# Loads of q and gates moved from ScalarE's to SyncE's queue, and the reload of the activation blocks spread over 24 projection steps, in a hybrid attention and retention layer

## The chip, the cores and the metric

The kernel runs on one core of a Trainium2 chip. The metric is device time in microseconds (us) of one execution; a time is the median of several. PE is TensorE, PEld its weight loads, DVE VectorE, ACT ScalarE, POOL GpSimd, SP SyncE. SPq and ACTq are the queues from which SyncE and ScalarE issue transfers.

## What is computed

One layer on 2048 latent tokens (a 32 x 64 grid) with 256 context tokens, width 1024. After an RMSNorm and a modulation, one input projection gives eight groups of columns: q, k, v and gate of a neighbourhood attention (8 heads of 64), and q, k, v and gate of a bidirectional retention (4 heads of 128). Both results are multiplied by their gates, joined, projected once more and added to the input.

```python
na_q, na_k, na_v, na_g, r_q, r_k, r_v, r_g = _split_proj(h_lat @ w_in)
o_na = _neighbourhood_attention(_heads(na_q, NA_HEADS), _heads(na_k, NA_HEADS),
                                _heads(na_v, NA_HEADS), k_na_ctx, v_na_ctx, na_rpb)
y_na = _merge(o_na) * jax.nn.silu(na_g)
o_ret = o_f + jnp.flip(o_b, 2)
y_ret = _head_rmsnorm(o_ret, ret_norm_g).astype(dt) * jax.nn.silu(r_g)
y_lat = jnp.concatenate([y_na, y_ret], axis=-1) @ w_out
x = x + gate * y_lat
```

In the attention each latent query reads, in one softmax, a clamped window of 8 rows and 16 columns of the grid with a learned bias, and all context keys.

## The kernel before

Products are made in float32r from two parts, a rounded value ("hi") and its remainder ("lo"), in three matmuls. The normalised activations h lie in five blocks: four of 512 latent tokens, and one of 256 context tokens. Each block has a tile `hhi` and a tile `hlo`.

The program has four stages. First the projections of the attention and part of the retention run block by block (`tform`, line 351, and `tokform`, line 361); their results go to DRAM (qS, kS, vS, vB, gS, and rkS, rvS, rqS for the retention). Blocks 2 and 3 of h are written to DRAM as well (hS), because their space is needed. Then comes the attention, tile by tile, with the remaining retention projections woven in. After it come the backward states of the retention, and last the forward retention with the output projection.

The attention loop (line 964) has 128 tiles, t = 16h + 4i + j: head h, block of eight grid rows i, block of sixteen columns j, and three more rounds at its end. One round makes the scores of tile t (`s_mm`, PE, line 755), their minimum with the bias (`s_min`, DVE, line 764), the exponential (`s_exp`, ACT, line 769), the normalisation of tile t−1 (`s_norm`, POOL, line 775), the transposes of tile t−2 into `tr` (`p_tr`, PE, lines 782 and 784), the copy of `tr` into `pt` (ACT, line 786) and its remainder (DVE, line 792), and the product of tile t−3 with v (`pv`, PE, lines 803 and 805). Every second tile is put together by `combine` (lines 826 to 834). On every fourth tile it multiplies by the gate `gt` on POOL and stores the result y in yS.

Between these steps stands `fill` (line 703). It advances a stream of projection steps, of which a unit (u_rk, u_rv, u_rq) has eight and ends with a store. Over the whole loop 384 − 66 = 318 such steps are shared out evenly among the 131 rounds; the 66 are held back for the stage behind. Each call of a step first takes one entry off the list `dmas` and issues it on SyncE; an entry may be `None`. `reload(b)` (line 622) fills this list with the loads of a block from hS: it is called for block 2 when the last step of the u_rq units of block 0 is done, and for block 3 after block 1, in the third pair of weight groups (line 691). From there 32 steps (two u_rk units and two u_rq units) pass before block b+2 is read.

At the end of each round loads for later tiles are issued: the q of the next row block (`load_q`, line 723, two buffers, two transfers each) at j = 0; the gate (`load_gate`, line 813, two buffers) at j = 1; groups of v (`load_v`, line 730, six buffers); the bias (`bias`, line 737, into `nb`); k and the context's v of the next head (`load_head`, line 715). The q of the next head is loaded at i = 3, j = 0. All of them go out on SyncE, but for q and the gate, which ACT issues. Stores go out on ACT too (line 149, put off by one or two rounds). The weights of the stream come into `st` (line 175), the rotary tables into `rot` (lines 402 and 405), both on SyncE.

The order of the instructions on an engine is that of the code. An engine that issues a transfer waits in its place until the transfer may go; what stands behind on that engine waits with it. The builder gives the transfers of both queues eight completion semaphores in turn, DMAHW0 to DMAHW7.

Of the kernel before, what the change touches and what calls it, by code (L numbers as in the profile page):

```python
# [81 lines left out]
def hybrid_kernel(ctx: ExitStack, tc: tile.TileContext, a: dict, out: bass.AP):  # L82
    nc = tc.nc
    f = lambda ap: ap[:].bitcast(F32)
# [6 lines left out]
    gS = [dram.tile([P, L], F32, name=f"gS{t}") for t in range(4)]  # L91
# [6 lines left out]
    hS = [[dram.tile([P, KC * 512], F32, name=f"hS{b}_{hl}") for hl in range(2)] for b in range(2)]  # L98
# [40 lines left out]
    def tick():  # L139
        for e in later:  # L140
            e[0] -= 1
        due = [e for e in later if e[0] <= 0]
        later[:] = [e for e in later if e[0] > 0]
        for e in due:
            e[1]()
# [10 lines left out]
    blk = [(hx.tile([P, KC, 512], F32R, name="hhi"), hx.tile([P, KC, 512], F32R, name="hlo"))] + [None] * 4  # L156
# [463 lines left out]
    dmas, chop = [], []  # L620

    def reload(b):
        blk[b] = (hx.tile([P, KC, 512], F32R, name="hhi"), hx.tile([P, KC, 512], F32R, name="hlo"))
        dmas.extend([None] * 3)
        for k in range(0, KC, 2):
            for hl in range(2):
                dmas.append((f(blk[b][hl])[:, k:k + 2, :].rearrange("p k t -> p (k t)"), hS[b - 2][hl][:, k * 512:(k + 2) * 512]))

    def fill_stream(w):
        def units(kind, b):  # L630
# [51 lines left out]
        for b in range(4):  # L682
            for n, args in enumerate(units(rk, b)):
                yield from steps(rk(w, ck, *args))
                late_load(n + 2 * b)
            if b == 3:
                w = next_c()
            for args in units(rq, b):
                yield from steps(rq(wn, cq, *args))
            if b < 2:  # L690
                reload(b + 2)
# [11 lines left out]
    def fill(n):  # L703
        for _ in range(n):
            if dmas:
                d = dmas.pop(0)
                if d:
                    nc.sync.dma_start(*d)
            if next(env["fill"], 0) == 0:
                return  # L710
# [12 lines left out]
    def load_q(hd, h, i):  # L723
        q = kp.tile([P, 2, 512], F32R, name="q", bufs=2)
        src = qS[h // 2][i, 64 * (h % 2):64 * (h % 2) + 64]
        for e in range(2):
            nc.scalar.dma_start(f(q)[64 * e:64 * e + 64], src)
        hd["q"][i] = q

    def load_v(hd, gs):  # L730
        for g in gs:
            vt, h = kp.tile([P, 4, P], F32R, name="vt", bufs=6), hd["h"]
            for e, n in ((0, P), (2, 96)):
                nc.sync.dma_start(f(vt)[:n, e:e + 2, :], vB[h // 4][:n, g, e:e + 2, (h % 4) * P:(h % 4 + 1) * P])
            hd["vt"][g] = vt

    def bias(h, rt, ct):
        n, o = BT[rt][ct]
        nc.sync.dma_start(nbz[int(rt == 1)][:, nbt[int(rt == 1), ct]:][:, :n], a["rpb_t"][h, :, o:o + n])
# [3 lines left out]
    def dims(t):  # L743
        h, i, j = t // 16, t // 4 % 4, t % 4
        return h, i, j, KWIN[i][0], KWIN[i][1], CWIN[j][0], CWIN[j][1]

    def s_mm(t):
        h, i, j, kr0, kr, kc0, cw = dims(t)
        hd, nk, odd = heads[h], kr * cw, t % 2
        pl = sS[:, 1024:1024 + nk] if odd else sS[:, 512 - nk:512]  # L750
        pc = sS[:, 768:1024] if odd else sS[:, 512:768]
        kg = hd["k2"][:, :L].rearrange("p (r c) -> p r c", c=GW)
        for o, k in ((pl, kg[:, kr0:kr0 + kr, kc0:kc0 + cw]), (pc, hd["k2"][:, L:])):
            for hl in range(2):
                nc.tensor.matmul(o, hd["q"][i][:, hl, j * P:(j + 1) * P], k, start=(hl == 0), stop=(hl == 1))  # L755
        tl_st[t] = dict(s=sS[:, 768:1024 + nk] if odd else sS[:, 512 - nk:768], nk=nk, lo=LC * odd, co=nk * (1 - odd),
                        sp=ap_.tile([P, 768], F32, name="sp", bufs=3), st=ap_.tile([P, 4], F32, name="stt", bufs=4))

    def s_min(t):
        h, i, j = dims(t)[:3]  # L760
        T = tl_st[t]
        n, big = T["nk"] + LC, int(RTYPE[i] == 1)
        o = nbt[big, CTYPE[j]] - T["lo"]
        nc.vector.tensor_tensor_reduce(T["sp"][:, :n], T["s"], nbz[big][:, o:o + n], -1.0, 3e38, ALU.add, ALU.min, T["st"][:, 0:1])  # L764

    def s_exp(t):
        T = tl_st[t]
        sp, st, n = T["sp"], T["st"], T["nk"] + LC
        nc.scalar.activation(sp[:, :n], sp[:, :n], AF.Exp, bias=st[:, 0:1], scale=-1.0, accum_out=st[:, 1:2])  # L769

    def s_norm(t):
        T = tl_st[t]
        sp, st, n = T["sp"], T["st"], T["nk"] + LC
        nc.vector.reciprocal(st[:, 2:3], st[:, 1:2])  # L774
        nc.gpsimd.tensor_scalar(sp[:, :n], sp[:, :n], st[:, 2:3], 0.0, ALU.mult, ALU.add)  # L775

    def p_tr(t):
        h, i, j, kr0, kr, kc0, cw = dims(t)
        T = tl_st[t]
        sp, nk, ng_, cn = T["sp"], T["nk"], kr // 4, 4 * cw  # L780
        for g in range(ng_):
            nc.tensor.transpose(tr[:cn, g, :], sp[:, T["lo"] + g * cn:T["lo"] + (g + 1) * cn], ident)  # L782
        for g in range(2):
            nc.tensor.transpose(tr[:, ng_ + g, :], sp[:, T["co"] + g * P:T["co"] + (g + 1) * P], ident)  # L784
        pt = ap_.tile([P, 6, 2, P], F32R, name="pt")
        nc.scalar.copy(pt[:, :ng_ + 2, 0, :], tr[:, :ng_ + 2, :])  # L786
        T.update(pt=pt, ng=ng_)

    def p_lo(t):
        T = tl_st[t]  # L790
        pt, n = T["pt"], T["ng"] + 2
        nc.vector.tensor_tensor(pt[:, :n, 1, :], tr[:, :n, :], f(pt)[:, :n, 0, :], ALU.subtract)  # L792
# [15 lines left out]
    gts = {}  # L808

    def fin_(h):  # L810
        return slice(0, 64) if h % 2 == 0 else slice(64, 128)

    def load_gate(t):
        h, i = dims(t)[:2]
        gts[t // 4] = ap_.tile([P, 512], F32, name="gt", bufs=2)
        nc.scalar.dma_start(gts[t // 4][fin_(h)], gS[h // 2][fin_(h), i * 512:(i + 1) * 512])

    def combine(t):
        h, i, j = dims(t)[:3]
# [47 lines left out]
    def decay_exp(dcol, c128):  # L867
        lg = rt["lg"]
        nc.scalar.activation(lg, lg, AF.Exp)
        nc.vector.tensor_scalar(lg, lg, -1.0, None, ALU.mult)  # L870
        for H in HS:
            for d in range(2):
                sc = lg[:, d * RH + H["r"]:d * RH + H["r"] + 1]
                nc.scalar.activation(H["w"][:, d:d + 1], dcol[:, d:d + 1], AF.Exp, scale=sc)
                nc.scalar.activation(H["w"][:, 2 + d:3 + d], c128, AF.Exp, scale=sc)
# [88 lines left out]
    for t in range(NT + 3):  # L964
        if t == 6:
            decay_exp(*dec)
        quota = (NF - held) * (t + 1) // (NT + 3) - done
        done += quota
        part = [quota // 3 + (quota % 3 > n) for n in range(3)]
        tick()  # L970
        if t < NT:
            s_mm(t)
        if 0 <= t - 1 < NT:
            s_norm(t - 1)
        fill(part[0])
        if t < NT:
            s_min(t)
        if 0 <= t - 2 < NT:
            p_tr(t - 2)
        if t < NT:  # L980
            s_exp(t)
        if 0 <= t - 2 < NT:
            p_lo(t - 2)
        fill(part[1])
        if 0 <= t - 3 < NT:
            pv(t - 3)
            if (t - 3) % 2 == 1:
                combine(t - 3)
        fill(part[2])
        if t >= NT:  # L990
            continue
        h, i, j = dims(t)[:3]
        hd = heads[h]
        if i == 0 and j < 3:
            bias(h, 1, j)
        if i == 2 and j < 3:
            bias(h, 2, j)
        if j == 1:
            load_gate(t)
        if i < 3 and j == 0:  # L1000
            load_q(hd, h, i + 1)
        for g in {(0, 2): (3,), (0, 3): (4,), (1, 1): (5,), (1, 3): (6,), (2, 3): (7,)}.get((i, j), ()):
            load_v(hd, (g,))
        if h + 1 < NH:
            if i == 1 and j == 2:
                heads[h + 1] = load_head(h + 1)
            if i == 3:
                nh = heads[h + 1]
                if j == 0:
                    load_q(nh, h + 1, 0)  # L1010
                if j == 1:
                    bias(h + 1, 0, 0)
                    load_v(nh, (0,))
                if j == 3:
                    bias(h + 1, 0, 1)
                    load_v(nh, (1, 2))
        if h > 0 and (i, j) == (0, 0):
            bias(h, 0, 2)
# [211 lines left out]
    q, r = divmod(48 - used, 7)  # L1230
    plan = [q + (n < r) for n in range(7)] + [15] * 8 + [10] * 4
    for s in range(NJ + 3):
        q = plan[s]
# [121 lines left out]
```

## Time and profile before

| | us |
|---|---|
| median of 3 runs (lowest, highest) | 1401.06 (1400.52, 1403.14) |
| the profiled execution | 1401.82 |
| its span, first to last instruction | 1400.0 |
| PE busy | 1346.2 |
| DVE busy | 641.3 |
| ACT busy | 530.9 |
| POOL busy | 493.3 |

The profile is that of one execution. A line of the timeline has start and length in us, engine, source line, operation, tile written and tiles read, partitions x elements, and count; the bracket at its end is the time that the engine stood idle before it, with what ended that. SPq and ACTq rows are transfers issued; their length is that of the issue, not of the transfer. In the chain of waits each row has start and length of one step of the chain that ended last; a DMA row there lasts from issue to landing. The granted clock of TensorE is a share of full speed, and the DMA share is the mean busy share of the core's 16 DMA engines.

### The profile page before, as it was taken

Reading aid. Unit: us, or ns where it says so; the run is one execution under the profiler, and the core shown is the slowest. Engines: PE = TensorE matmul, PEld = TensorE weight load, DVE = VectorE, ACT = ScalarE, POOL = GpSimd, SP = SyncE. Lnnn points to the kernel's source line nnn. Section 1 sums busy time; section 2 is a strip of 40 time slices with the busy share of each in tenths; the row PEclk is TensorE's granted clock in tenths of the full one; section 3 lists DMA queues with packets and bytes.
Section 4 is the critical chain, followed back from the end, with each engine's and each line's share of the span. In section 5 each row is a group of like instructions: output and inputs, shape, how many; then the busy total and the mean of one; then the engine's idle time right before and its main releaser. Section 6 shows DMA issues by size and latency. Waiting matters only on the chain.

```text
span 1400.0 us, 22749 instructions
## 1 busy us (share of the span) xinstructions
PE 1346.2 (96%) x8380; PEld 1176.6 (84%) x8380; DVE 641.3 (46%) x1244; ACT 530.9 (38%) x1155; POOL 493.3 (35%) x499
## 2 busy tenths in 40 slices
PE   6999999999999999999999998899999999999997
PEld 2477899988887888899899898798999779888886
DVE  5787211100021131467776766676663643344445
ACT  4454312122112121555556544346552234333332
POOL 4352402022110221344554433346343155454342
PEclk9999999999999999999999999999999999999999
DMA  9543578743154678758768696966636898555533
GB/s 312 171 151 121 191 251 276 223 136 105 48 170 132 217 259 265 201 151 209 207 166 213 190 276 183 257 182 172 185 110 224 269 312 269 183 167 172 158 114 128
DMA packets 218705, 270.45 MB, mean 193 GB/s; under 512 B 16865, under 2 KB 163425, under 8 KB 217570
## 3 DMA queue, kind: packets, MB, share of 16 engines
q1 hardware_dynamic: 175106, 184.30, 44.3%
q10 hardware_dynamic: 43488, 84.69, 18.8%
q8 instruction: 67, 1.10, 0.3%
q14 instruction: 44, 0.36, 0.1%
HBM read 179.80 MB, written 89.13 MB: 192 GB/s over the span
## 4 chain that ended last, share of the span: by engine, by line
PE 77%; DMA 8%; DVE 6%; issue 3%; ACT 2%; POOL 2%; SPq 1%; ACTq 0%; POOLq 0%; DVEq 0%
PE mm L357 25%; PE mm L368 19%; PE mm L1199 12%; PE sS L755 4%; PE tr L782 3%; PE po L803 3%; PE mm L922 2%; PE mm L301 2%; PE tr L784 2%; PE po L805 1%; DMA q<-qS 1%; DMA hlo<-hS 1%; DMA vt<-vB 1%; DMA v<-rvS 1%; PE mm L1111 1%
## 5 line engine op out<-in xcount | busy, mean ns | idle before, releaser
L357 PE MATMUL mm<-hhi,whi 128*128 128x512 f32 x640 | 260.3, 407 | 0.0
L357 PE MATMUL mm<-hlo,whi 128*128 128x512 f32 x640 | 254.0, 397 | 5.4 <-DVE hlo L254 2.1
L357 PE MATMUL mm<-hhi,wlo 128*128 128x512 f32 x640 | 254.0, 397 | 0.2 <-DVE wlo L338 0.2
L368 PE MATMUL mm<-whi,hhi 128*128 128x256 f32 x768 | 224.2, 292 | 0.0
L368 PE MATMUL mm<-wlo,hhi 128*128 128x256 f32 x768 | 216.7, 282 | 2.7 <-POOL wlo L338 2.7
L368 PE MATMUL mm<-whi,hlo 128*128 128x256 f32 x768 | 215.5, 281 | 0.0
L338 POOL TENSOR_TENSOR wlo<-st,whi 128x256 fp32r<-128x256 f32 (+1 forms) x97 | 112.1, 1171 | 243.2 <-ACT whi L336 240.2
L786 ACT CAST pt<-tr 128x640 fp32r<-128x640 f32 (+1 forms) x128 | 95.6, 747 | 201.8 <-PE tr L784 167.6
L792 DVE TENSOR_TENSOR pt<-tr,pt 128x640 fp32r<-128x640 f32 (+1 forms) x128 | 113.9, 890 | 104.9 <-ACT pt L786 104.1
L368 PEld LDWEIGHTS mm<-wlo,hhi 128*128 128x128 f32 x768 | 144.6, 188 | 3.4 <-POOL wlo L338 3.3
L357 PEld LDWEIGHTS mm<-hlo,whi 128*128 128x128 f32 x640 | 121.2, 189 | 30.8 <-issue 2.5
L357 PEld LDWEIGHTS mm<-hhi,whi 128*128 128x128 f32 x640 | 121.1, 189 | 29.5 <-issue 5.4
L357 PEld LDWEIGHTS mm<-hhi,wlo 128*128 128x128 f32 x640 | 120.8, 189 | 29.5 <-DVE wlo L338 0.6
L368 PEld LDWEIGHTS mm<-whi,hlo 128*128 128x128 f32 x768 | 144.9, 189 | 0.0
L368 PEld LDWEIGHTS mm<-whi,hhi 128*128 128x128 f32 x768 | 144.8, 189 | 0.0
L775 POOL TENSOR_SCALAR sp<-sp,stt 128x640 f32<-128x640 f32 (+2 forms) x128 | 103.2, 808 | 113.2 <-DVE stt L774 76.8
L764 DVE CUSTOM_DVE_ANT_0 sp<-sS,nb 128x640 f32<-128x640 f32 (+2 forms) x128 | 105.6, 825 | 21.8 <-PE sS L755 14.0
L769 ACT ACTIVATE sp<-sp,stt 128x640 f32<-128x640 f32 (+2 forms) x128 | 107.5, 839 | 15.4 <-DVE stt L764 15.0
L755 PE MATMUL sS<-k,q 128*128 128x256 f32 (+3 forms) x512 | 99.0, 315 | 4.6 <-DVE stt L764 4.2
L1199 PE MATMUL mm<-wor,y 128*128 128x512 f32 x384 | 95.9, 398 | 0.9 <-DVE xt L1208 0.7
L755 PEld LDWEIGHTS sS<-k,q 128*128 128x128 f32 x512 | 83.8, 189 | 11.4 <-DVE stt L764 6.6
L1199 PE MATMUL mm<-won,y 128*128 128x512 f32 x336 | 89.9, 406 | 0.0
(214 smaller groups left out, 2238.5 us busy)
## 6 DMA issues: line engine op xcount, KB each, us to landing
st<-in_w_in_dram SPq DMA_DIRECT2D x48, 512.0 KB
q<-qS ACTq DMA_DIRECT2D x64, 256.0 KB
k<-kS SPq DMA_DIRECT2D x16, 576.0 KB
kS<-o SPq DMA_DIRECT2D x16, 512.0 KB
woS<-g ACTq DMA_DIRECT2D x32, 256.0 KB
qS<-o ACTq DMA_DIRECT2D x16, 512.0 KB
vt<-vB SPq DMA_DIRECT2D x64, 128.0 KB
k<-rkS SPq DMA_DIRECT2D x32, 256.0 KB
```

The source lines that it names most:

```text
L338: eng.tensor_tensor(l, r, f(h), ALU.subtract)
L357: nc.tensor.matmul(pm[:, :n], ww[:, k, cs], h[:, k, :], start=(k == 0 and i == 0), stop=(k == KC - 1 and i == 2))
L368: nc.tensor.matmul(pm[:, t * WG:(t + 1) * WG], h[:, k, o:o + P], ww[:, k, :], start=(k == 0 and i == 0), stop=(k == KC - 1 and i == 2))
L755: nc.tensor.matmul(o, hd["q"][i][:, hl, j * P:(j + 1) * P], k, start=(hl == 0), stop=(hl == 1))
L764: nc.vector.tensor_tensor_reduce(T["sp"][:, :n], T["s"], nbz[big][:, o:o + n], -1.0, 3e38, ALU.add, ALU.min, T["st"][:, 0:1])
L769: nc.scalar.activation(sp[:, :n], sp[:, :n], AF.Exp, bias=st[:, 0:1], scale=-1.0, accum_out=st[:, 1:2])
L775: nc.gpsimd.tensor_scalar(sp[:, :n], sp[:, :n], st[:, 2:3], 0.0, ALU.mult, ALU.add)
L782: nc.tensor.transpose(tr[:cn, g, :], sp[:, T["lo"] + g * cn:T["lo"] + (g + 1) * cn], ident)
L786: nc.scalar.copy(pt[:, :ng_ + 2, 0, :], tr[:, :ng_ + 2, :])
L792: nc.vector.tensor_tensor(pt[:, :n, 1, :], tr[:, :n, :], f(pt)[:, :n, 0, :], ALU.subtract)
L803: nc.tensor.matmul(po[:, t % 2, :, :], hd["vt"][kr0 // 4 + g][:cn, VORD.index(j), :], pt[:cn, g, :, :], start=(g == 0), stop=False)
L1199: nc.tensor.matmul(pm, yy[:, k, :], ww[:, k, sl], start=(k == 0 and i == 0), stop=(k == 3 and i == 2))
```

## The change

Three things change. The two transfers of `load_q` and that of `load_gate` are issued by SyncE. `reload` puts two empty entries ahead of each of its eight pieces, in place of three ahead of the first: the pieces go out at steps 3, 6, ... 24 after the call, where they went out at steps 4 to 11. And at the end of a round the q load stands first, ahead of the bias, while the gate's load stands behind the v groups and is issued one tile later, at j = 2.

```diff
     def reload(b):
         blk[b] = (hx.tile([P, KC, 512], F32R, name="hhi"), hx.tile([P, KC, 512], F32R, name="hlo"))
-        dmas.extend([None] * 3)
         for k in range(0, KC, 2):
             for hl in range(2):
-                dmas.append((f(blk[b][hl])[:, k:k + 2, :].rearrange("p k t -> p (k t)"), hS[b - 2][hl][:, k * 512:(k + 2) * 512]))
+                dmas.extend([None, None, (f(blk[b][hl])[:, k:k + 2, :].rearrange("p k t -> p (k t)"), hS[b - 2][hl][:, k * 512:(k + 2) * 512])])
...
         for e in range(2):
-            nc.scalar.dma_start(f(q)[64 * e:64 * e + 64], src)
+            nc.sync.dma_start(f(q)[64 * e:64 * e + 64], src)
...
-        nc.scalar.dma_start(gts[t // 4][fin_(h)], gS[h // 2][fin_(h), i * 512:(i + 1) * 512])
+        nc.sync.dma_start(gts[t // 4][fin_(h)], gS[h // 2][fin_(h), i * 512:(i + 1) * 512])
...
+        if i < 3 and j == 0:
+            load_q(hd, h, i + 1)
         if i == 0 and j < 3:
             bias(h, 1, j)
         if i == 2 and j < 3:
             bias(h, 2, j)
-        if j == 1:
-            load_gate(t)
-        if i < 3 and j == 0:
-            load_q(hd, h, i + 1)
         for g in {(0, 2): (3,), (0, 3): (4,), (1, 1): (5,), (1, 3): (6,), (2, 3): (7,)}.get((i, j), ()):
             load_v(hd, (g,))
+        if j == 2:
+            load_gate(t)
```

In the changed kernel the lines behind `reload` have numbers that are lower by one: what is line 786 before is line 785 there. The order of PE's, DVE's and POOL's work, and of ACT's computing instructions, is the same.

## The prediction

> **What bounds the kernel now.** I read the page first: engine line, then the shares of the chain.
>
> ```profile
> PE 1346.2 (96%) x8380; PEld 1176.6 (84%) x8380; DVE 641.3 (46%) x1244; ACT 530.9 (38%) x1155; POOL 493.3 (35%) x499
> PE 77%; DMA 8%; DVE 6%; issue 3%; ACT 2%; POOL 2%; SPq 1%; ACTq 0%; POOLq 0%; DVEq 0%
> ```
>
> TensorE is busy for 1346.2 of 1400.0 us, and no matmul is added or removed. The change can only return idle time of PE, or time at a lower clock. So the next view was the windows, over the attention stage that the change touches (columns: length, then busy time and count of PE, PEld, DVE, ACT, POOL; granted clock; DMA share; GB/s).
>
> ```profile
> 700.00:800.00 100.00, 98.56 (x758) 94.16 (x757) 69.45 (x155) 55.29 (x114) 48.87 (x56) 1.00 0.70 188
> 800.00:900.00 100.00, 91.46 (x634) 84.82 (x633) 63.94 (x147) 42.49 (x84) 36.26 (x38) 0.95 0.86 241
> 900.00:1000.00 100.00, 96.85 (x718) 90.91 (x717) 70.36 (x155) 54.30 (x113) 47.36 (x55) 1.00 0.67 191
> ```
>
> The middle row is the odd one: PE idles 8.54 us there against 1.44 just before, the clock is 0.95, and the DMA engines are at 0.86. The waits before PE's instructions in that stretch, from the timeline, with the engine that ended each:
>
> ```profile
> 844.01 1.09 PE L782 MATMUL tr<-ident,sp 128*128 128x128 f32 x4 [4.32 <-DVE pt L792]
> 874.48 0.52 PE L782 MATMUL tr<-ident,sp 128*128 128x128 f32 x3 [0.39 <-DVE pt L792]
> 876.53 0.59 PE L803 MATMUL po<-pt,vt 96*128 96x256 f32 x3 [0.60 <-ACT pt L786]
> 879.10 0.55 PE L782 MATMUL tr<-ident,sp 128*128 128x128 f32 x3 [0.33 <-POOL sp L775]
> 885.55 0.97 PE L755 MATMUL sS<-k,q 128*128 128x512 f32 x4 [0.27 <-DVE stt L764]
> 889.86 1.06 PE L782 MATMUL tr<-ident,sp 128*96 128x128 f32 x4 [2.63 <-DVE pt L792]
> 906.43 0.97 PE L755 MATMUL sS<-k,q 128*128 128x512 f32 x4 [1.37 <-DVE stt L764]
> ```
>
> Together 9.91 us. DVE's pt (L792) follows ACT's copy of pt (L786), so I asked what ACT did before the two large ones (ACTq rows are transfers that ACT issues):
>
> ```profile
> 829.97 0.45 ACTq L727 DMA_DIRECT2D q<-qS  x1
> 839.55 0.45 ACTq L816 DMA_DIRECT2D gt<-gS  x1
> 841.60 0.38 ACTq L149 DMA_DIRECT2D rkS<-o  x1
> 842.07 0.80 ACT L786 CAST pt<-tr 128x768 fp32r<-128x768 f32 x1 [7.12 <-DMA gt<-gS]
> ...
> 883.60 4.47 ACTq L727 DMA_DIRECT2D q<-qS  x2
> 888.17 0.69 ACT L786 CAST pt<-tr 128x640 fp32r<-128x640 f32 x1 [4.78 <-DMA rot<-in_rot_s_dram]
> ```
>
> ACT stands still for 7.12 us and for 4.78 us around its own issues of q and gate loads, with the pt copy behind them. The chain of waits says for what:
>
> ```profile
> 829.97 9.56 DMA q<-qS
> 839.53 0.02 issue
> 839.55 2.52 DMA gt<-gS
> ```
>
> The gate's load was issued 0.02 us after a q load landed that had been issued 9.56 us earlier. The program's order gives the reason. Its transfers, SyncE's and ACT's alike, count on semaphores DMAHW0 to DMAHW7 in turn, and one waits until the last of its number has landed. These are ACT's rows at that place before (head 4, second block of rows; y is the finished tile, o a projection's output):
>
> ```order
> L149 DMA yS_85<-y_7465 64x512 [waits DMAHW0_49,Pool_49]
> L786 CAST pt<-tr 128x6x128 [waits DVE_49,PE_49]
> L769 ACTIVATE sp,stt<-sp,stt 128x640 [waits DVE_49]
> L826 COPY cmb<-po 64x256 [waits PE_49]
> L727 DMA q<-qS_59 64x1024 [waits DMAHW4_49,DMAHW2_49]
> L727 DMA q<-qS_59 64x1024 [waits DMAHW4_49]
> L786 CAST pt<-tr 128x6x128 [waits DVE_49,PE_49]
> L769 ACTIVATE sp,stt<-sp,stt 128x768 [waits DVE_49]
> L816 DMA gt<-gS_71 64x512 [waits DMAHW2_49]
> L149 DMA rkS_78<-o 128x2x256 [waits DMAHW3_49,Pool_49]
> L786 CAST pt<-tr 128x6x128 [waits DVE_49,PE_49]
> ```
>
> The same place after the change:
>
> ```order
> L149 DMA yS_85<-y_7464 64x512 [waits DMAHW4_49,Pool_49]
> L785 CAST pt<-tr 128x6x128 [waits DVE_49,PE_49]
> L768 ACTIVATE sp,stt<-sp,stt 128x640 [waits DVE_49]
> L825 COPY cmb<-po 64x256 [waits PE_49]
> L785 CAST pt<-tr 128x6x128 [waits DVE_49,PE_49]
> L768 ACTIVATE sp,stt<-sp,stt 128x768 [waits DVE_49]
> L149 DMA rkS_78<-o 128x2x256 [waits DMAHW3_49,Pool_49]
> L785 CAST pt<-tr 128x6x128 [waits DVE_49,PE_49]
> ```
>
> The q and gate loads are gone from ACT; the store rkS still stands ahead of the pt copy, with a landing to wait for.
>
> **Part 1, loads of q and gates on SyncE.** Their counts and durations (min/median/max ns):
>
> ```profile
> L727 ACTq DMA_DIRECT2D q<-qS x64: 452/476/1360, 544.4 to 1020.6; - x64
> L816 ACTq DMA_DIRECT2D gt<-gS x32: 452/452/512, 570.4 to 1037.6; - x32
> ```
>
> 64 × 0.476 + 32 × 0.452 = 45 us of issuing leaves ACT for SyncE's queue, spread over 476 us, a tenth of it; neither is on the chain (SPq 1%). Bytes are the same. What counts is the waits. Removed: both holds above, so PE's 4.32 and 2.63 us = 6.95. On SyncE a q load waits for its buffer, which PE's scores of the tile just before have left, so what is queued behind it (bias, v groups, k of the next head) waits at most until PE has reached that place in the program; the score, value and bias steps that need those loads come later still. A gate goes out one tile later than before and is needed four tiles on. Four tiles take 14.8 us, by two score rows four tiles apart:
>
> ```profile
> 815.60 0.88 PE L755 MATMUL sS<-k,q 128*128 128x512 f32 x4
> 830.40 0.87 PE L755 MATMUL sS<-k,q 128*128 128x512 f32 x4
> ```
>
> That covers the slowest landing that I found, the 11.90 below. If the cover goes, PE waits for the difference.
>
> **Part 2, the reload.** Eight pieces of 512 KB per block, first and last issue of each block before:
>
> ```profile
> 809.76 0.47 SPq L708 DMA_DIRECT2D hhi<-hS  x1
> 824.48 1.14 SPq L708 DMA_DIRECT2D hlo<-hS  x1
> 865.25 0.38 SPq L708 DMA_DIRECT2D hhi<-hS  x1
> 886.18 0.32 SPq L708 DMA_DIRECT2D hlo<-hS  x1
> 868.47 11.90 DMA hlo<-hS
> ```
>
> SyncE's order from the first piece, before:
>
> ```order
> L708 DMA hhi<-hS_0_87 128x1024
> L734 DMA vt<-vB_68 128x2x128
> L734 DMA vt<-vB_68 96x2x128
> L708 DMA hlo<-hS_1_88 128x1024
> L708 DMA hhi<-hS_0_87 128x1024
> L708 DMA hlo<-hS_1_88 128x1024
> L708 DMA hhi<-hS_0_87 128x1024
> L734 DMA vt<-vB_68 128x2x128
> L734 DMA vt<-vB_68 96x2x128
> L708 DMA hlo<-hS_1_88 128x1024
> L708 DMA hhi<-hS_0_87 128x1024
> L405 DMA rot<-in_rot_c_dram 128x512
> ```
>
> and after, from the same piece:
>
> ```order
> L707 DMA hhi<-hS_0_87 128x1024
> L733 DMA vt<-vB_68 128x2x128
> L733 DMA vt<-vB_68 96x2x128
> L707 DMA hlo<-hS_1_88 128x1024
> L726 DMA q<-qS_59 64x1024 x2
> L733 DMA vt<-vB_68 128x2x128
> L733 DMA vt<-vB_68 96x2x128
> L707 DMA hhi<-hS_0_87 128x1024
> L405 DMA rot<-in_rot_c_dram 128x512
> L405 DMA rot<-in_rot_s_dram 128x512
> L815 DMA gt<-gS_71 64x512
> ```
>
> Three pieces now stand ahead of the rotary load (rot), where seven stood, and a q load has come in among them. The tile loop takes 384 − 66 = 318 steps in 131 rounds, 2.43 a tile, so 24 steps are 9.9 tiles or 37 us. The pieces are used from step 33 on, the last from step 36: 12 steps or 18 us after its issue, more than 11.90. So the same bytes, at a lower peak and nearer to the stretch's mean share of 0.86. I count no gain of its own here: it is what shortens the landings for which ACT's remaining stores wait.
>
> **The clock.** After the two large waits the clock column falls:
>
> ```profile
> 840.00:844.00 4.00, 0.00 (x0) 0.02 (x1) 0.96 (x1) 1.90 (x4) 0.00 (x0) 0.73 0.88 257
> 844.00:848.00 4.00, 3.99 (x16) 3.71 (x17) 3.21 (x8) 1.81 (x4) 2.59 (x3) 0.50 0.35 102
> 848.00:852.00 4.00, 4.00 (x26) 3.70 (x26) 3.02 (x6) 1.67 (x4) 1.68 (x2) 0.91 0.18 51
> 888.00:892.00 4.00, 2.14 (x8) 1.95 (x9) 3.01 (x7) 1.69 (x4) 1.51 (x2) 0.71 1.09 188
> 892.00:896.00 4.00, 4.00 (x24) 3.57 (x23) 2.98 (x8) 2.02 (x4) 1.59 (x2) 0.87 1.12 225
> ```
>
> (1 − clock) × 4 us over the rows with work: 2.00 + 0.36 after the first wait, 1.16 + 0.52 after the second, 4.04 us in all; the 0.73 of the first row falls into idle time. The Trainium skill (TensorE: Matmul & The Clock Gate, "HAM oscillation — how this bites in real kernels") warns of idle gaps of PE over about 3.4 us as what drops the clock. By it only the 4.32 wait would cost clock, 2.36 us, and the gain below would be 1.68 smaller; the trace differs, 0.71 right behind a wait of 2.63, and I go by the trace.
>
> **The sum.** Removed: 4.32 + 2.63 + 4.04 = 10.99. Kept: the store rkS, issued at 841.60, 1.60 after the gate's issue ended (839.55 + 0.45), so with a wait of its own that this change does not take away. Its bounds are 0 and 1.60; I keep all 1.60, since the store's place ahead of the pt copy is unchanged. The five small waits (2.96 us) I leave as they are: DVE and POOL end three of them. Gain 9.4. The profiled execution took 1401.82 (span 1400.0), so 1392.4 for it; it stood 0.76 above the median of 1401.06, so 1391.7 for the median. Upper bound of the gain: all 9.91 and 4.04, and the 900 to 1000 row brought from 3.15 idle down to the 1.44 of 700 to 800, is 15.7: 1385.4.
>
> **Rivals.** *One hold stays* (0.20). The stores are still on ACT and still wait for a landing eight transfers back, now always one of SyncE's. If the larger hold only moves to the rkS store, the gain is the second alone, 2.63 + 1.68 = 4.3: 1396.8. For it: the 1.60 above. Against: fewer reload bytes stand ahead of it.
>
> *Nothing moves* (0.13). The transfers are the same, and so is their sum. If the DMA engines, at 0.86 over the whole stretch, set the pace there, the landings stay as late as they are and every wait goes to the stores, or to DVE through rotary and bias loads: 1401. The Trainium skill (DMA: Bandwidth & Descriptors, "Issuing engines are not separate DMA queues") speaks for this: the issuing engine doesn't matter to the transfers, and choosing it only saves issue time. By that the change is worth no more than issue time off the chain, nothing. Against: 0.70 and 0.67 on either side, 0.18 at 848 to 852, so there is room to spread into; and what ACT loses in the trace is no issue time but a wait in front of its copies.
>
> *Slower: q comes too late* (0.14). In one queue q stands behind reload pieces. The place is the q load of tile 84, right behind the first piece of the second block; the other one shown is that of tile 72, behind the second piece of the first block (pieces, then the scores that need q):
>
> ```profile
> 811.26 0.45 SPq L708 DMA_DIRECT2D hlo<-hS  x1
> 826.34 0.75 PE L755 MATMUL sS<-k,q 128*128 128x384 f32 x4
> 877.20 0.85 PE L755 MATMUL sS<-k,q 128*128 128x384 f32 x4
> ```
>
> From 865.25 to 877.20 are 11.95 us; less two issues of 0.476, 11.0 remain. A landing of 9.56 fits, one of 11.90 is 0.9 late, and each further piece that q waits behind adds its own landing. It decides where q lands more than 11.0 after that piece. The price is that of the holds now: scores late by some 2.5 us with 1.7 of clock, once per block, on top of holds that stay: 2 × 4.2 = 8.4, 1409.5. Against: tile 72 has 15.08, and with the burst gone a landing of 11.90 is the exception.
>
> **How the numbers follow.** The forecast has 0.53, one hold 0.20, nothing 0.13, slower 0.14. 0.2% (2.8 us) is about what a measurement of this kernel can tell from no change; the three runs before spread over 2.6. The first two lie beyond it: faster 0.73, same 0.13, slower 0.14. The range runs from 1385.4 to 1405, into the slower case up to a single late q per run (4.2), and leaves out most of the 0.14 and little else. The likeliest case alone has 1387 to 1395.
>
> **What would show it.** Right: no ACT idle of over 4 us before L785 between 800 and 900, clock 1.00 there, PE idle in that row down from 8.54 to about 2, DMA share in 20 us windows without the swing. Wrong: a wait before L785 ended by a transfer with the rkS or yS store's issue just ahead (one hold stays); DMA share and landings unchanged (nothing moves); a wait of PE before L754, ended by q, or before L367 by hlo (slower, or the reload too late). A gain outside 800 to 910 would mean that I looked at the wrong stretch.

## The result, and the profile after

| | before | after |
|---|---|---|
| median, us (lowest to highest) | 1402.10 (1400.52 to 1405.03) | 1389.31 (1387.86 to 1389.82) |
| ratio to before, 95% interval | 1 | 0.9910 (0.9892 to 0.9929) |
| the profiled execution, us | 1401.82 | 1387.86 |
| its span, us | 1400.0 | 1386.1 |

The change saves 12.8 us, 0.9%. The forecast was 1391.7, a gain of 9.4. First the two lines of the page after, TensorE's and the shares of the chain:

```profile
PE 1339.7 (97%) x8380; PEld 1172.7 (85%) x8380; DVE 641.4 (46%) x1244; ACT 530.6 (38%) x1155; POOL 494.2 (36%) x499
PE 79%; DVE 7%; DMA 5%; issue 3%; POOL 3%; ACT 2%; SPq 1%; POOLq 0%; ACTq 0%; DVEq 0%
```

The work of each engine is the same; the part of transfers in the chain fell from 8% to 5%. The busy time of PE is 6.5 us less for the same 8380 instructions; 4.6 us of that lie in the attention stage, where TensorE no longer runs at half clock. The windows of the attention stage after (length, then busy time and count of PE, PEld, DVE, ACT, POOL; granted clock; DMA share; GB/s):

```profile
700.00:800.00 100.00, 99.27 (x763) 95.13 (x762) 68.09 (x151) 56.32 (x117) 47.68 (x55) 1.00 0.70 195
800.00:900.00 100.00, 98.09 (x705) 91.22 (x702) 73.65 (x165) 48.36 (x94) 41.95 (x43) 1.00 0.92 254
900.00:1000.00 100.00, 98.23 (x758) 93.95 (x757) 69.29 (x154) 56.49 (x118) 47.32 (x55) 1.00 0.65 185
```

The odd row is no longer odd: PE idles 1.91 us there, not 8.54, at clock 1.00, not 0.95, and 705 of PE's instructions fit into it where 634 did. Its DMA share is higher than before, 0.92. In pieces of 20 us:

```profile
800.00:820.00 20.00, 20.00 (x160) 19.54 (x158) 15.65 (x35) 10.73 (x21) 8.60 (x9) 1.00 0.68 201
820.00:840.00 20.00, 19.14 (x134) 17.46 (x133) 14.32 (x33) 9.16 (x17) 8.93 (x9) 1.00 1.00 275
840.00:860.00 20.00, 20.00 (x147) 18.77 (x146) 14.97 (x34) 9.99 (x20) 7.63 (x8) 1.00 0.84 227
860.00:880.00 20.00, 19.61 (x147) 18.46 (x147) 14.28 (x35) 9.25 (x20) 7.82 (x8) 1.00 1.02 304
880.00:900.00 20.00, 19.34 (x125) 16.98 (x123) 14.44 (x31) 9.23 (x17) 8.96 (x9) 1.00 1.04 264
```

Before, the share in the same pieces was 0.78, 1.06, 0.55, 0.83, 1.07. The DMA engines are still full in three of five. What went is the hole of 0.55 that followed PE's standstill; as I read it, a kernel that stands still asks for nothing. The waits of PE in the stretch, from the timeline (the bracket is the idle time, with what ended it):

```profile
839.16 0.74 PE L754 MATMUL sS<-k,q 128*128 128x288 f32 x4 [0.86 <-DMA q<-qS]
868.91 0.55 PE L781 MATMUL tr<-ident,sp 128*128 128x128 f32 x3 [0.36 <-POOL sp L774]
890.53 0.98 PE L754 MATMUL sS<-k,q 128*128 128x512 f32 x4 [0.66 <-DVE stt L763]
905.23 0.72 PE L802 MATMUL po<-pt,vt 128*128 128x256 f32 x4 [0.94 <-DVE y L828]
```

The last one stands in the trace before as well, at 921.11, behind the rows that the prediction shows; so 9.91 + 0.94 = 10.85 us became 2.82. Both large waits in front of tr, the 4.32 and the 2.63, are gone. One new wait has come, 0.86 us for a q. ACT's own waits between 800 and 900 (engine, tile and line, what it waited for: us in all, times, longest):

```profile
ACT pt L785 <- PE tr L783: 45.0, 26, 2.7
ACT sp L768 <- DVE stt L763: 2.9, 5, 1.2
ACT pt L785 <- DVE stt L773: 2.4, 1, 2.4
```

No transfer is among them, so ACT is nowhere held in this stretch; it waits for PE, which is as it should be where PE is the bound. Where the new wait of PE comes from stands in the chain of waits:

```profile
819.23 10.67 DMA rkS<-o
829.90 0.02 issue
829.92 0.32 SPq L707
...
830.34 0.45 SPq L726
830.79 0.04 issue
830.83 8.20 DMA q<-qS
839.03 0.14 issue
839.16 0.74 PE sS L754 x4
```

ACT's store of rkS took 10.67 us to land. SyncE stood at its next reload piece until then (in the program that piece waits for DMAHW1, on which the store counts), and the q load behind it went out late. It is the hold of the kernel before, on the other queue, and there it cost PE 0.86 us.

Where the time came from: the attention stage from its first score to its last (the figures behind the durations, 564.9 to 1042.7 before) became 12.7 us shorter. These are the scores' groups, before and after:

```profile
L755 PE MATMUL sS<-k,q x512: 276/290/506, 564.9 to 1042.7; 128*128 128x256 f32 x86, 128*128 128x384 f32 x44, 128*128 128x512 f32 x21, 128*128 128x288 f32 x20
```

```profile
L754 PE MATMUL sS<-k,q x512: 276/289/504, 561.6 to 1026.7; 128*128 128x256 f32 x86, 128*128 128x384 f32 x44, 128*128 128x512 f32 x21, 128*128 128x288 f32 x20
```

477.8 against 465.1. The windows of the stage, before and after:

```profile
564.90:1043.00 478.10, 460.83 (x3448) 436.72 (x3447) 319.82 (x715) 256.98 (x538) 215.37 (x244) 0.99 0.71 195
```

```profile
561.60:1027.00 465.40, 456.20 (x3448) 433.28 (x3447) 319.93 (x715) 257.09 (x538) 215.96 (x244) 1.00 0.72 202
```

For the same 3448 instructions PE's idle time fell from 17.27 to 9.20 us, by 8.1, and its busy time from 460.83 to 456.20, by 4.6; together 12.7. The idle part is the waits above, 10.85 − 2.82 = 8.0. Of the busy part, 4.04 are the work at half clock that the prediction's rows show; 0.6 stay without a cause. The two profiled executions also differ ahead of the stage, by 3.3 us, where before has two short stretches at clock 0.5, at 39.7 and at 77.3 us. Another execution of the same kernel, below, has neither, so this is not counted for the change; behind the stage after is 2.1 us longer.

### The profile page after: what moved, and what is told of

Read it like the earlier page. It is cut to its first block, busy times and chain, and to the rows that moved or that the text cites. A ratio compares the mean times of both kernels' runs of the same rounds, so it can differ in the third digit from the quotient of the medians.

```text
span 1386.1 us, 22777 instructions
## 1 busy us (share of the span) xinstructions
PE 1339.7 (97%) x8380; PEld 1172.7 (85%) x8380; DVE 641.4 (46%) x1244; ACT 530.6 (38%) x1155; POOL 494.2 (36%) x499
## 4 chain that ended last, share of the span: by engine, by line
PE 79%; DVE 7%; DMA 5%; issue 3%; POOL 3%; ACT 2%; SPq 1%; POOLq 0%; ACTq 0%; DVEq 0%
PE mm L357 26%; PE mm L368 19%; PE mm L1198 11%; PE sS L754 4%; PE tr L781 3%; PE po L802 3%; PE mm L921 2%; PE tr L783 2%; PE po L804 2%; PE mm L301 1%; PE mm L1110 1%; PE mm L1109 1%; PE mm L1108 1%; DMA v<-rvS 1%; PE mm L1089 1%
## 5 line engine op out<-in xcount | busy, mean ns | idle before, releaser
L754 PE MATMUL sS<-k,q 128*128 128x256 f32 (+3 forms) x512 | 98.5, 314 | 4.4 <-DVE stt L763 3.4
L754 PEld LDWEIGHTS sS<-k,q 128*128 128x128 f32 x512 | 83.4, 188 | 11.2 <-DVE stt L763 5.5
```

## The experiments

**The theory to test** was that of the prediction: the queue is what matters, for ACT can't be held by loads that it doesn't issue, and spreading the reload gives nothing by itself. **The rival**: the burst of the reload is the cause of all the waits, and the queue only decides which engine feels it. Ratios are to the kernel before, measured beside it, with 95% intervals; a gain in us is (1 − ratio) times 1401.

**The kernel before once more**, a single run with a profile and no edit.

> The kernel before, unchanged, for a second profile. The first one has two drops of the clock in its first 100 us that the changed kernel's profile does not have. If they come by chance, this profile differs from the first in them and in nothing else; its attention stage should have the same two long waits of PE (4.3 and 2.6 us) within some tenths.

It took 1402.71 us. The larger wait is there again, 3.89 us, and the second one, before the same tr, was 4.12 where the first profile has 2.63:

```profile
840.06 1.08 PE L782 MATMUL tr<-ident,sp 128*128 128x128 f32 x4 [3.89 <-DVE pt L792]
887.64 1.06 PE L782 MATMUL tr<-ident,sp 128*96 128x128 f32 x4 [4.12 <-DVE pt L792]
```

So these holds belong to the kernel. From one execution to the other PE's waits differ by 0.4 and 1.5 us, the second by more than I had expected.

**The reload spread alone**: q and gates stay on ACT, at their old places.

```diff
-        dmas.extend([None] * 3)
...
-                dmas.append((f(blk[b][hl])[:, k:k + 2, :]...
+                dmas.extend([None, None, (f(blk[b][hl])[:, k:k + 2, :]...
```

> Only the reload is spread over 24 steps; q and gate loads stay on ACT, in their old places. Theory A (what costs is that ACT waits in line, ahead of its pt copies, for a transfer to land): ACT still issues 96 loads, so holds of ACT remain, though shorter; 1396 to 1400 us, a gain of 2 to 6, PE idle between 800 and 900 us of 4 to 6. Rival B (what costs is the burst of reload traffic, and the queue does not matter): nearly the whole gain, 1389 to 1392 us, PE idle under 2.5.

1394.4 us (1393.12 to 1395.27), 0.9958 (0.9946 to 0.9970): a gain of 5.9 us by a part that the prediction had put at nothing. The first block's hold of ACT has shrunk to 2.70 us and costs PE nothing; the second block's is still there. ACT's row there, and PE's two waits that follow:

```profile
876.96 0.69 ACT L785 CAST pt<-tr 128x640 fp32r<-128x640 f32 x1 [4.86 <-DMA rkS<-o]
```

```profile
878.65 0.61 PE L781 MATMUL tr<-ident,sp 128*96 128x128 f32 x4 [2.31 <-DVE pt L791]
887.83 1.41 PE L754 MATMUL sS<-k,q 128*128 128x384 f32 x4 [2.99 <-DMA q<-qS]
```

The chain of waits joins them:

```profile
868.91 7.47 DMA rkS<-o
876.39 0.02 issue
876.41 11.29 DMA q<-qS
```

The store, issued at 868.91, landed at 876.39; the second transfer of the q load had to wait for that (both count on DMAHW7), with pt behind it, and then took 11.29 us itself. PE's scores could start at 887.83. Spreading lowers the peak but leaves the coupling.

**The loads on SyncE alone**, at the new places, the reload in 8 steps.

```diff
-            nc.scalar.dma_start(f(q)[64 * e:64 * e + 64], src)
+            nc.sync.dma_start(f(q)[64 * e:64 * e + 64], src)
...
-        nc.scalar.dma_start(gts[t // 4][fin_(h)], ...
+        nc.sync.dma_start(gts[t // 4][fin_(h)], ...
...
+        if i < 3 and j == 0:
+            load_q(hd, h, i + 1)
...
-        if j == 1:
-            load_gate(t)
-        if i < 3 and j == 0:
-            load_q(hd, h, i + 1)
...
+        if j == 2:
+            load_gate(t)
```

> Only the q and gate loads are moved to SyncE, in their new places; the reload goes out in the old eight steps. Theory A: both large holds go, 1389 to 1393 us, PE idle between 800 and 900 us under 3. Rival B: the burst still delays landings and the stores on ACT wait for them, 1396 to 1401 us. Rival C (in one queue q comes too late behind the burst): PE waits before its score matmuls (L755) at a tile of a new row block, 1400 us or more.

1393.91 us (1389.00 to 1401.05), 0.9951 (0.9935 to 0.9966): 6.9 us, not the 9.4 that the prediction took for this part. The eleven executions are far apart, and the profiled one, at 1396.23, is among the slower ones. In it ACT waits for no transfer between 800 and 900. PE does:

```profile
842.49 0.39 PE L803 MATMUL po<-pt,vt 96*128 96x256 f32 x1 [2.15 <-DMA vt<-vB]
843.85 0.74 PE L755 MATMUL sS<-k,q 128*128 128x288 f32 x4 [0.72 <-DMA q<-qS]
889.11 0.93 PE L755 MATMUL sS<-k,q 128*128 128x384 f32 x4 [2.07 <-DMA q<-qS]
```

Three waits, 4.94 us, where the two holds had cost 6.95: with the burst still there, most of what ACT no longer waits for, PE waits for itself. This is the mechanism of the rival in which q comes too late.

**The new places alone**: the same moves within the round, but everything stays on ACT and the reload in 8 steps.

```diff
+        if i < 3 and j == 0:
+            load_q(hd, h, i + 1)
         if i == 0 and j < 3:
             bias(h, 1, j)
...
-        if j == 1:
-            load_gate(t)
-        if i < 3 and j == 0:
-            load_q(hd, h, i + 1)
...
+        if j == 2:
+            load_gate(t)
```

> Only the places within a round change (q ahead of the bias, gate behind the v groups and one tile later); both stay on ACT, the reload in eight steps. Theory A and rival B alike: no change, 1399 to 1403 us, since ACT waits at nearly the same point.

1405.43 us (1399.78 to 1408.02), 1.0028 (1.0015 to 1.0041): a little slower, where I had expected no change. ACT is now held four times for a transfer, for 3.7 to 7.9 us, and the largest wait of PE falls just behind 900, as the window and PE's row show:

```profile
900.00:1000.00 100.00, 93.11 (x665) 86.61 (x664) 66.76 (x146) 50.99 (x106) 46.40 (x53) 0.97 0.66 180
```

```profile
906.96 1.06 PE L782 MATMUL tr<-ident,sp 128*96 128x128 f32 x4 [4.93 <-DVE pt L792]
```

So the places bring nothing of the gain.

**The issuing engine alone**: the two words `nc.scalar` become `nc.sync` in `load_q` and `load_gate`; old places, reload in 8 steps.

```diff
-            nc.scalar.dma_start(f(q)[64 * e:64 * e + 64], src)
+            nc.sync.dma_start(f(q)[64 * e:64 * e + 64], src)
...
-        nc.scalar.dma_start(gts[t // 4][fin_(h)], ...
+        nc.sync.dma_start(gts[t // 4][fin_(h)], ...
```

> The kernel before, with the q and gate loads issued by SyncE, but at their old places in the round; the reload in 8 steps as before. If it is the issuing engine that counts, this is worth what the loads on SyncE at their new places were: 0.9951 (0.9935 to 0.9966), 1393 to 1396 us, no hold of ACT, and PE waits of 0.5 to 2 us before L755 ended by q. If the earlier place of q within the round is what makes that work, q now lands later behind bias and v groups, PE waits 2 to 4 us before L755 and the ratio is over 0.997.

1391.56 us (1389.01 to 1394.33), 0.9934 (0.9915 to 0.9953): 9.2 us. PE again waits for q, once per block, 3.30 us in all, where with the new places it waited 2.79 for q and 2.15 for vt:

```profile
840.56 0.74 PE L755 MATMUL sS<-k,q 128*128 128x288 f32 x4 [1.73 <-DMA q<-qS]
885.35 0.82 PE L755 MATMUL sS<-k,q 128*128 128x384 f32 x4 [1.57 <-DMA q<-qS]
```

It is the engine that counts, not the place. The earlier place of q brings no gain here; the intervals of 6.9 and 9.2 us overlap, so it can't be said to harm either. The Trainium skill (DMA: Bandwidth & Descriptors, "Issuing engines are not separate DMA queues") says that spreading transfers over issuing engines saves only the time to issue them. Taken for this move, that would mean no gain. Here the issue time is about 45 us and off the chain, and the change of engine was worth 9.2 us: the measurement decides. What that section leaves out is the wait of an engine in front of a transfer, with its computing instructions behind it.

**Without the reload**, before and after. Blocks 2 and 3 read the tiles of blocks 0 and 1 again; this leaves the 8 MB of reload out of the work, and the retention's second half gets other values.

```diff
-        blk[b] = (hx.tile([P, KC, 512], F32R, name="hhi"), hx.tile([P, KC, 512], F32R, name="hlo"))
-        dmas.extend([None] * 3)
...
+        blk[b] = blk[b - 2]
```

> The kernel before, with q and gates on ACT, but without the reload: blocks 2 and 3 of the woven projections read blocks 0 and 1 again, so their values are others and 16 transfers of 512 KB are left out; PE's work is the same. If the reload's traffic is the root and ACT's queue only the place where it is felt (rival B in a weaker form): all long waits go, 1387 to 1390 us. If waiting in ACT's line costs by itself (theory A): some holds stay, 1392 to 1396.

> The changed kernel without the reload (blocks 2 and 3 of the woven projections read blocks 0 and 1 again, so values differ and 16 transfers of 512 KB are left out). It is the floor of what a better reload could bring. If the spread reload is hidden: 1387 to 1390 us, as the changed kernel. If it still costs: 1385 or less.

Before without it: 1390.0 us (1388.56 to 1391.20), 0.9916 (0.9887 to 0.9944). After without it: 1388.1 us (1386.53 to 1391.79), 0.9909 (0.9881 to 0.9937). The windows, before without reload first:

```profile
800.00:900.00 100.00, 98.92 (x708) 91.93 (x707) 74.52 (x166) 50.04 (x98) 41.09 (x42) 1.00 0.66 181
```

```profile
800.00:900.00 100.00, 98.89 (x709) 91.81 (x707) 74.28 (x167) 48.50 (x94) 41.95 (x43) 1.00 0.65 178
```

With q and gates on ACT, and every store too, all long waits go as soon as the reload is gone: PE idles 1.08 us in the stretch and the DMA share is 0.66. This settles the root. The holds need the burst; without it ACT's queue costs nothing that these runs could show (0.9916 on ACT, 0.9909 on SyncE). And it gives the floor: the changed kernel, at 0.9910 with the whole reload, is where the kernels without it are. Of the reload's price of about 12 us nothing measurable is left.

**Half the spreading**: the changed kernel with one empty entry ahead of each piece, 16 steps in place of 24.

```diff
-                dmas.extend([None, None, (f(blk[b][hl])...
+                dmas.extend([None, (f(blk[b][hl])...
```

> The changed kernel, but the reload goes out over 16 steps in place of 24: one empty entry ahead of each piece. If it is the peak of traffic that counts, 4.2 MB in some 25 us in place of 37 us, some of the waits come back: PE idle of 2.5 to 5 us between 800 and 900 and a ratio of 0.992 to 0.994, between 0.991 of the change and 0.9951 of the loads alone with 8 steps. If any spreading suffices, it is 0.991 or below with PE idle of 1 to 2 us.

1393.33 us (1390.51 to 1395.62), 0.9945 (0.9924 to 0.9965). Worse than I had expected (0.992 to 0.994): no better than the 0.9951 of 8 steps. The second block runs clean, the first has the largest single wait of all kernels with the loads on SyncE. Its chain, and PE's row:

```profile
823.34 10.90 DMA k<-kS
834.24 0.02 issue
834.26 0.02 SPq L726
...
834.80 9.31 DMA q<-qS
```

```profile
844.25 1.25 PE L754 MATMUL sS<-k,q 128*128 128x288 f32 x4 [6.61 <-DMA q<-qS]
```

The q load could not go out before a k load of the next head had landed (in the program it waits for DMAHW6, on which that load counts), 10.90 us after its issue, and then needed 9.31. Two landings in a row take 20 us; from the k load's issue to the time when the scores were due (844.25 − 6.61 = 837.64) there were 14.3. The same place cost 0.86 us with 24 steps. As I read this one trace, it isn't enough to spread: each landing has to stay short enough that two of them fit.

**The variations around the change.** Three more kernels ask whether anything is left: q and gates at their old places, on SyncE, with the reload in 24 steps; the change with the attention stage's stores on SyncE as well, so that ACT issues nothing there; and both. The edits to the changed kernel, places first, then stores:

```diff
-        if i < 3 and j == 0:
-            load_q(hd, h, i + 1)
...
+        if j == 1:
+            load_gate(t)
+        if i < 3 and j == 0:
+            load_q(hd, h, i + 1)
...
-        if j == 2:
-            load_gate(t)
```

```diff
     done, held = 0, 66
+    env["queue"] = nc.sync
...
+    env["queue"] = nc.scalar
     flush()
     atx.close()
```

> The changed kernel with the old places within a round: the gate ahead of the v groups and at j = 1, q behind the bias, all on SyncE, the reload over 24 steps. The two parts and the places alone measured 0.9958, 0.9951 and 1.0028 of before, both parts together 0.991. If the places cost 0.2 to 0.3% on SyncE too, as they did on ACT: 1385 to 1388 us. If they matter only where ACT waits in line: the changed kernel's time, 1388 to 1390. If q ahead of the bias is what brings q in time on SyncE: slower, 1391 or more, with waits of PE for q before its score matmuls.

> The changed kernel with the stores of the attention stage on SyncE as well, so that ACT issues no transfer there. If what is left of the waits comes from stores in ACT's line: 1385 to 1388 us. If SyncE, now held up by stores that wait for POOL's and DVE's results, gets its loads out too late: 1392 us or more, with waits of PE ended by q or v loads. If nothing is left to gain: 1388 to 1390.

> The changed kernel with q and gates at their old places, on SyncE, and the stores of the attention stage on SyncE as well. If both variations of the last runs (0.9896 and 0.99 against 0.991) are worth something and add up, this gives 0.988 to 0.9893, 1384 to 1387 us. If the change already sits at the floor that the kernel without the reload shows (0.9909), it is 0.989 to 0.992 and not to be told from the changed kernel.

> The changed kernel once more, beside the others on one chip: 0.991 (0.989 to 0.993). A value of 0.9896 or below would mean that the old places were worth nothing and that the earlier difference came from chip and rounds.

| kernel | median, us | ratio (95% interval) |
|---|---|---|
| old places on SyncE | 1386.99 | 0.9896 (0.9867 to 0.9926) |
| stores on SyncE | 1388.16 | 0.9900 (0.9869 to 0.9931) |
| both | 1386.68 | 0.9899 (0.9879 to 0.9919) |
| the change, beside "both" | 1388.24 | 0.9911 (0.9891 to 0.9931) |

Every interval holds the others' values. "Both" is 1.56 us below the change on the same chip, a tenth of a per cent; none is shown to beat it. Their windows, in the order of the first three, say the same:

```profile
800.00:900.00 100.00, 98.90 (x709) 91.86 (x708) 74.03 (x167) 48.51 (x95) 41.93 (x43) 1.00 0.91 253
```

```profile
800.00:900.00 100.00, 98.90 (x711) 92.07 (x710) 73.29 (x165) 49.39 (x96) 41.63 (x43) 1.00 0.95 260
```

```profile
800.00:900.00 100.00, 98.89 (x715) 92.23 (x714) 73.59 (x163) 48.74 (x95) 41.13 (x42) 1.00 0.96 257
```

1.1 us of idle time each, as without any reload. The second profile of the change has 1.12 there and no wait for q: the 0.86 of the first comes and goes.

All together, as ratios (the change is the last entry of the row of 24 steps):

| reload in | q, gates on ACT, old places | on SyncE, old places | on SyncE, new places |
|---|---|---|---|
| 8 steps | 1 | 0.9934 | 0.9951 |
| 16 steps | | | 0.9945 |
| 24 steps | 0.9958 | 0.9896 | 0.9910, 0.9911 |
| no reload | 0.9916 | | 0.9909 |

Spreading alone 5.9 us, the loads alone 6.9 or, at the old places, 9.2 us, both 12.6 to 12.8, and the floor without the reload about 12. So each half gives a part, and both together reach the floor; whether the halves simply add up can't be told beside it. Neither theory holds as it was put. The rival is right about the root: the burst is the cause. But the queue does more than decide which engine feels it: with the whole burst, the issuing engine alone took away 9.2 us of about 12.

What stays open: how much of a late landing is traffic and how much is the wait on a semaphore that another queue's transfer holds. More semaphores, or one set for each queue, would tell; that wasn't tried. Nor is it settled whether the old places are 0.1% better on SyncE.

## Why the prediction was right, and where it was not

**What bounds it, and where.** Right. All of the gain lies in the attention stage, between 800 and 920 us; PE's idle time elsewhere in that stage is 6.4 us before and after.

**ACT's holds.** Right in mechanism: both are gone, whenever q and gates leave ACT (four kernels, with the reload in 8 or 24 steps, show no wait of ACT for a transfer between 800 and 900).

**"Removed: both holds above, so PE's 4.32 and 2.63 us"** as the result of Part 1. This step failed in its size. Alone the part gives 6.9 us (4.8 to 9.1), with the clock, not 10.99 less 1.60: the waits come back on PE as 2.15, 0.72 and 2.07. With the old places it gives 9.2, near the forecast's 9.4, but PE waits for q there too, 3.30 us. The fault is in its cover. The prediction set four tiles, 14.8 us, against the slowest landing, 11.90, and so took for granted that SyncE would issue q on time. SyncE issues wait for landings as ACT's did: for a store of 10.67 us in the change, a k load of 10.90 with 16 steps. The time from the place in the program to the landing is the sum of a wait and a landing, and that sum is what has to be held against the cover.

**"I count no gain of its own here"**, of Part 2. Wrong: 5.9 us alone, and without it the change would have stayed at 0.9951. The half sentence behind it, that it shortens the landings for which others wait, was the real effect, and had no number. The row to price it by stood in the prediction: 188 to 191 GB/s at a share of 0.70 and 0.67 on either side of the stretch, where PE idles 1.4 to 3.2 us per 100. With the reload's bytes taken out the stretch could be expected to look like these rows, and so 5.4 to 7.1 of the 8.54 to be the burst's; the run without the reload has 7.5.

**The clock.** About right: 4.04 was taken, and PE's busy time in the stage fell by 4.6. The mean clock of 0.95 over 100 us would give 5, but it counts the half clock within the idle time too, where it costs nothing.

**The sum.** Forecast 9.4, measured 12.8. Waits: 6.95 − 1.60 forecast, 8.0 measured. The hold that the rkS store was to keep, 1.60, didn't stay; in place of the five small waits (2.96) there are two, of 1.02 together; the new one for q costs 0.86. That is 6.95 + 1.94 − 0.86 = 8.0. Two errors met: 9.4 for the loads, which alone gave 6.9, and nothing for the reload, which alone gave 5.9. That they cancelled in part is luck. Two slips in the working moved little: DVE and POOL end four of the five small waits, not three, and the upper bound counts the wait of 1.37 at 906.43 twice, once in the 9.91 and once in the row of 900 to 1000. Without that it is 14.3, or 1386.8 us.

**The rivals.** That one hold stays: no, ACT is not held between 800 and 900. That nothing moves: no; the DMA engines, 0.92 busy in the stretch, had the room. That q comes too late: its mechanism is real, once per block at 0.72 to 2.07 with 8 steps and once at 6.61 with 16, but the kernel was never slower than before for it. The prediction priced it on top of holds that stay, and they don't stay: the same move that makes q late frees ACT.

**The signs.** No ACT idle ended by a transfer, clock 1.00, PE idle 1.91 where about 2 was announced: as said. A DMA share "without the swing" was not: it still reads 0.68 to 1.04, since the same bytes go through a stretch that is as full as before. One sign of being wrong did show, in small: a wait of PE before L754 ended by q, 0.86 us.

## What to carry to other kernels

When an engine that computes also issues transfers, look for idle time of it in front of a computing instruction that is ended by a transfer: its own issue ahead of that was waiting for somebody else's landing. Moving the issue to another queue frees that engine, but the load can then be late for whoever needs it, unless what makes landings long, here 8 MB in two bursts, is spread as well. Before pricing either remedy, take the burst out altogether in one run: it shows the floor, and whether the two remedies share one gain or each hold a part of it.

## What the runs showed of the hardware

The clock of TensorE fell after shorter waits than I had thought. In the attention stage, over eight profiles, each wait of 3.89 us or more (3.89, 4.12, 4.32, 4.93, 6.61) came with 6.8 to 6.9 us at half clock, which began some 1 to 2 us before the wait ended, and those of 2.63, 2.79 and 2.99 came with 3.4 us. Waits of 1.73 us and less that stand alone came with none. In between it goes both ways: 2.15 and 2.31 came with none, 2.07 twice with 3.4 us at half clock, once with another wait of 1.31 just ahead of it. Four windows: behind the 2.99 with the reload spread alone, behind the 2.07 with the loads alone, and behind the 1.73 and the 1.57 with the issuing engine alone.

```profile
888.00:892.00 4.00, 4.00 (x17) 3.47 (x18) 0.83 (x2) 0.58 (x1) 0.00 (x0) 0.65 1.06 283
```

```profile
890.00:894.00 4.00, 4.00 (x18) 3.42 (x17) 1.37 (x3) 1.37 (x2) 0.00 (x0) 0.62 1.04 274
```

```profile
840.00:844.00 4.00, 3.44 (x23) 3.16 (x24) 2.60 (x6) 1.32 (x2) 1.56 (x2) 1.00 0.61 173
885.00:889.00 4.00, 3.65 (x24) 3.34 (x25) 1.45 (x3) 1.45 (x3) 0.23 (x1) 1.00 1.01 278
```

The Trainium skill (TensorE: Matmul & The Clock Gate, "HAM oscillation — how this bites in real kernels") puts the limit at idle gaps of more than about 3.4 us. In these traces all five waits above it cost clock, and some of those from 2.07 us on did too.
